# Twelve value column tiles of a gated linear attention layer by seven block products (Strassen) a pair, ahead of the heads

## The chip, the cores and the metric

The kernel runs on one core of one Trainium2 chip. The metric is the device time of one execution in microseconds (us). Five engines work beside each other, each through its own instructions in a fixed order: TensorE (PE: matmuls; PEld: the loading of their weights), VectorE (DVE), ScalarE (ACT), GpSimd (POOL) and SyncE (SP). SP's and POOL's queues also issue the transfers (DMA) between DRAM and the on-chip memory SBUF; matmuls write into PSUM. Engines wait for each other by semaphores.

## The reference

An encoder of two layers over 512 tokens of 2048 values, with 16 learned meta tokens ahead of them (528 columns in all). Each layer is h <- h + post_norm(mixer(pre_norm(h))). Layer 0 mixes by softmax attention. Layer 1 mixes by gated linear attention, with four heads, 256 key and 512 value channels each; what concerns the change is its input projection:

```python
proj = hp @ w_in          # w_in: 2048 x 6176
q, k, v, g_out, lr_f, lr_b = jnp.split(proj, [1024, 2048, 4096, 6144, 6160], axis=-1)
q = heads(q, GLA_HEAD_K) * (GLA_HEAD_K ** -0.5)
k, v = heads(k, GLA_HEAD_K), heads(v, GLA_HEAD_V)
o = o_f + o_b             # two gated scans over chunks, forward and backward
o = rmsnorm(o, o_norm)
return (o * jax.nn.silu(g_out)) @ w_out
```

All of it is float32. The values are 2048 columns of w_in: sixteen column tiles of 128.

## The kernel before

The kernel is one program, written out as Python. Activations lie with channels on the partitions and tokens along the free axis: u is 16 tiles (k = 0 to 15) of 128 x 528. A float32 product is made of three matmuls of a reduced kind: each operand is split into a high part (rounded, by a copy on ScalarE) and a low part (the rest, by a subtraction on VectorE), and hi x hi, hi x lo and lo x hi are added up in PSUM (split(), L130 to L132; three(), L153 to L156). uh and ul are the parts of u; weights() (L143) loads 512 KB of weights into a tile named wraw, of which there are two, and splits it into whi and wlo, of which there are three each, some 400 priorities ahead of the place where it stands.

project() (L158) makes one column tile of 128: in HALVES (twice 264 tokens) it is 2 x 16 x 3 = 96 matmuls of 264, in REAL (the 512 real tokens) 48 of 512. group() (L171) makes two column tiles at once in four banks of PSUM, with other work (extra) in each step k.

The order is set in two steps. A Clock in the Python program keeps a modelled time: project(), group() and the heads advance it, and side work, registered by clk.after() or as a generator by clk.drive(), is written out when the modelled time reaches it; clk.finish() writes out the rest of a generator at once. Then the framework orders the instructions of each engine by priorities; what stands in that order is fixed in the built program.

Around the change the work runs like this. At the end of layer 0 the output projection makes h tile by tile; squares() has ScalarE square each tile and GpSimd add it into acc (L649), mean_rsqrt() forms the norm (L661), and residual() (L665) makes h, in halves, and from it uh and ul. group() (L750) then makes the first two key tiles of layer 1 in ten steps that are split by halves, with the low-rank columns (plr) and the residual of the next tiles in it; token_major() (L695) transposes h (ht) and sums its squares by token. second_norm() (L760) makes the norm of layer 1: five small matmuls (mrow, L769) spread it over all partitions, each copied by ScalarE into r1row (L770), since all of them use one PSUM tile in turn. project() of the first q tile runs beside it, then lrf (L779) splits the low-rank columns by direction.

Then come four heads. Each makes two key and two query tiles (kf and qf, scaled by the norm: take_k L753, take_q L756), four value tiles (value_tile(), L964: project, copy to vt, transposes vps, copies times the norm into vh and vl) and four tiles of the output gate (gate_tile(), L990). Beside them go, as generators, gates() (L818: decays from the low-rank columns by the matmuls pz, L829), scores() (L872: chunk by chunk decayed queries and keys and their products, one item each "slot" of modelled us) and, a head later, outputs(). The normed, gated outputs go to DRAM (og_d), and the output projection ends the program.

## Time and profile before

| | us |
|---|---|
| runs (3), median | 1809.86 |
| runs, lowest to highest | 1809.09 to 1812.7 |
| the profiled execution | 1808.54 |
| its span, first to last instruction | 1806.8 |
| TensorE busy | 1784.1 (12855 matmuls) |
| VectorE / ScalarE / GpSimd busy | 1000.9 / 896.3 / 163.3 |
| mean granted TensorE clock | 0.998 |
| head 1 of layer 1 | 1151.24 to 1314.22, 163.0 long |

How to read it: a row of the timeline gives start, length, engine, line, operation and tile, and in brackets how long the engine stood idle before and what ended that. Starts count from the first instruction. Matmuls are pipelined, so their lengths overlap; the step from start to start is what one costs. A group's row gives its busy time and the mean length in ns, and behind the second bar the idle time ahead of its instructions. A row of the waits gives the line that waited, what ended the wait, the total in us, the times and the longest. A row of a stretch gives, for each engine, busy us and the number of instructions, then the granted clock, the share of DMA engines in use and GB/s. The page's rows of transfers end with the median us from issue to landing.

### The profile page before, as it was taken

The numbers are of one execution on the slowest core, as the hardware profiler recorded it, in microseconds if no ns is written. First come the engines' busy times: TensorE is split into PE (matmuls) and PEld (weight loads), VectorE is DVE, ScalarE is ACT, GpSimd is POOL, SyncE is SP. The second block draws the span as 40 slices with busy tenths as digits, with TensorE's granted clock in tenths as the row PEclk, the third lists the DMA queues.
The fourth block names the chain that finished last, engine by engine and source line by source line (L and its number), as shares of the span: only waits on it lengthen the run. The fifth ranks groups of instructions, "written<-read, shape, count | busy, mean of one in ns | idle before, by whom it ended". The sixth has DMA issues, their size and how long they took to land.

```text
span 1806.8 us, 31956 instructions
## 1 busy us (share of the span) xinstructions
PE 1784.1 (99%) x12855; PEld 1683.8 (93%) x12855; DVE 1000.9 (55%) x1985; ACT 896.3 (50%) x1869; POOL 163.3 (9%) x185
## 2 busy tenths in 40 slices
PE   8999999999999999999999999999999999999998
PEld 8899999999999999999999898998999899988886
DVE  5776565656565656632255575565456465654224
ACT  4555444444444454542346575566447454743221
POOL 3211111111111111211110000000000000000000
PEclk9999999999999999999999999999999999999999
DMA  8322223323233332433435232323223333434333
GB/s 273 103 67 76 84 87 86 91 80 91 81 91 84 91 113 81 143 106 93 117 118 174 71 84 80 94 73 92 80 85 85 92 88 91 126 117 175 93 94 128
DMA packets 262133, 184.24 MB, mean 102 GB/s; under 512 B 8460, under 2 KB 238160, under 8 KB 261456
## 3 DMA queue, kind: packets, MB, share of 16 engines
q1 hardware_dynamic: 257312, 165.78, 31.8%
q0 software_dynamic: 4672, 16.42, 2.5%
q8 instruction: 101, 1.65, 0.4%
q14 instruction: 48, 0.39, 0.1%
HBM read 156.03 MB, written 19.64 MB: 97 GB/s over the span
## 4 chain that ended last, share of the span: by engine, by line
PE 92%; DVE 2%; ACT 2%; DMA 1%; POOL 1%; issue 1%; SPq 0%; DVEq 0%; POOLq 0%; ACTq 0%
PE pp L154 22%; PE pp L156 22%; PE pp L155 21%; PE f L1057 2%; PE f L1055 2%; PE f L1056 2%; PE pT L492 2%; PE s L473 1%; PE s L474 1%; PE s L475 1%; PE o L935 1%; ACT whi L131 1%; PE o L934 1%; PE o L933 1%; DMA qs<-qw 1%; PE o L513 1%
## 5 line engine op out<-in xcount | busy, mean ns | idle before, releaser
L154 PE MATMUL pp<-uh,whi 128*128 128x264 f32 (+1 forms) x3024 | 913.4, 302 | 2.1 <-ACT acc L644 1.0
L156 PE MATMUL pp<-uh,wlo 128*128 128x264 f32 (+1 forms) x3024 | 903.1, 299 | 0.4 <-POOL wlo L279 0.3
L155 PE MATMUL pp<-ul,whi 128*128 128x264 f32 (+1 forms) x3024 | 901.4, 298 | 0.3 <-DVE ul L340 0.3
L154 PEld LDWEIGHTS pp<-uh,whi 128*128 128x128 f32 x3024 | 569.1, 188 | 20.7 <-ACT acc L644 1.2
L156 PEld LDWEIGHTS pp<-uh,wlo 128*128 128x128 f32 x3024 | 569.4, 188 | 17.1 <-POOL wlo L279 0.6
L155 PEld LDWEIGHTS pp<-ul,whi 128*128 128x128 f32 x3024 | 569.8, 188 | 16.1 <-DVE ul L340 0.5
L132 DVE TENSOR_TENSOR wlo<-wraw,whi 128x1024 fp32r<-128x1024 f32 (+1 forms) x254 | 310.1, 1222 | 366.1 <-ACT whi L131 360.7
L131 ACT CAST whi<-wraw 128x1024 fp32r<-128x1024 f32 (+1 forms) x254 | 264.3, 1042 | 405.0 <-PE pp L155 278.8
L482 ACT ACTIVATE pn<-s,mx 128x528 f32<-128x528 f32 (+1 forms) x72 | 50.3, 699 | 88.4 <-DVE mx L479 66.9
L1057 PE MATMUL f<-whi,ul 128*128 128x512 f32 x192 | 75.6, 394 | 0.0
L1055 PE MATMUL f<-whi,uh 128*128 128x512 f32 x192 | 75.5, 393 | 0.0
L1056 PE MATMUL f<-wlo,uh 128*128 128x512 f32 x192 | 75.3, 392 | 0.0
L225 POOL TENSOR_TENSOR qw<-qw,cos 128x528 f32<-128x528 f32 x24 | 31.8, 1326 | 372.8 <-DMA qs<-qw 339.0
L478 DVE TENSOR_REDUCE mx<-s 128x1 f32<-128x528 f32 (+1 forms) x72 | 50.8, 705 | 18.9 <-PE s L475 17.8
L960 POOL DMA_DIRECT2D og_d<-og x24 | 12.8, 542 | 492.9 <-DVE og L958 492.9
L497 DVE TENSOR_TENSOR pl<-pT,ph 128x512 fp32r<-128x512 f32 (+1 forms) x80 | 47.5, 593 | 4.8 <-ACT ph L496 3.8
L235 DVE TENSOR_TENSOR qw<-qw,qs 128x528 f32<-128x528 f32 x24 | 17.0, 707 | 59.2 <-POOL qs L226 59.2
L496 ACT CAST ph<-pT 128x512 fp32r<-128x512 f32 (+1 forms) x80 | 40.6, 507 | 16.2 <-PE pT L492 10.1
L1057 PEld LDWEIGHTS f<-whi,ul 128*128 128x128 f32 x192 | 36.1, 188 | 8.3
L1056 PEld LDWEIGHTS f<-wlo,uh 128*128 128x128 f32 x192 | 36.1, 188 | 8.3
L1055 PEld LDWEIGHTS f<-whi,uh 128*128 128x128 f32 x192 | 36.1, 188 | 8.1
L860 DVE TENSOR_TENSOR eq<-eq,qf 128x512 f32<-128x512 f32 (+1 forms) x56 | 34.4, 614 | 15.7 <-ACT eq L858 14.8
(335 smaller groups left out, 2766.0 us busy)
## 6 DMA issues: line engine op xcount, KB each, us to landing
wraw<-in_gla_w_in_dram SPq DMA_DIRECT2D x96, 512.0 KB, 3.9
wraw<-in_attn_w_in_dram SPq DMA_DIRECT2D x94, 512.0 KB, 3.9
wraw<-in_attn_w_out_dram SPq DMA_DIRECT2D x32, 512.0 KB, 3.8
wraw<-in_gla_w_out_dram SPq DMA_DIRECT2D x32, 512.0 KB, 3.8
qs<-qw SPq DMA_DIRECT2D x96, 66.0 KB, 2.8
h<-h_d SPq DMA_DIRECT2D x32, 132.0 KB, 2.4
h_d<-h POOLq DMA_DIRECT2D x16, 256.0 KB, 3.5
h_d<-hb SPq DMA_DIRECT2D x16, 256.0 KB, 2.8
```

Source lines behind the costliest of these rows:

```text
L131: A.copy(hi, src)
L132: V.tensor_tensor(lo, src, hi.bitcast(F32), op=ALU.subtract)
L154: PE.matmul(ps, wh, uh[:, k, a:b], start=first, stop=False)
L155: PE.matmul(ps, wh, ul[:, k, a:b], start=False, stop=False)
L156: PE.matmul(ps, wl, uh[:, k, a:b], start=False, stop=last)
L478: V.reduce_max(mx, s, axis=AX.XY)
L482: A.activation(pn[:, :T].rearrange("p (a b) -> p a b", a=2), s, AF.Exp, bias=mx, scale=SCALE, accum_out=sm)
L496: A.copy(ph[:, :, c:c + m], pt[:, :, qc:qc + m])
L497: V.tensor_tensor(pl[:, :, c:c + m], pt[:, :, qc:qc + m], ph[:, :, c:c + m].bitcast(F32), op=ALU.subtract)
L1055: PE.matmul(ps, uh[:, k, ts], wh[:, kk], start=(k == 0), stop=False)
L1056: PE.matmul(ps, uh[:, k, ts], wl[:, kk], start=False, stop=False)
L1057: PE.matmul(ps, ul[:, k, ts], wh[:, kk], start=False, stop=(k == KT - 1))
```

## The change

Strassen's scheme (in Winograd's form) makes a product of 2 x 2 blocks with seven block products in place of eight. Here the blocks are two column tiles of w_in (256 columns) by the two halves of the 2048 channels on one side, and the two halves of the channels by the two halves of the 528 tokens on the other. So a pair of value tiles takes seven products of 8 x 3 = 24 matmuls of 264, 168 in all.

What is new or moved:

- residual() also writes h to DRAM (hf_d), by GpSimd's queue, 32 transfers of 128 x 264.
- group() makes the first two value tiles, not the first two key tiles; ScalarE copies them to y tiles (four copies).
- combine() forms, once, the sums of blocks of u that the products need, T1 to T4: for each k of 8 it loads two tiles of h (three transfers), scales them on ScalarE, makes three subtractions on VectorE, and splits the result, 128 x 1056, into th and tl. It goes beside the first and second key tile and the first query tile, in four tiles x0 to x3 (in the build x_12374 to x_12377).
- seven() makes a pair: it loads four quarters of the weights (a11, a21, a22, a12, 512 KB each) into the tiles of a list of six (those four and two of wraw), forms three sums of them on VectorE ahead and one behind (L236), splits each product's weights, and makes the products (matmuls L242 to L244); the sums of the results go to the y tiles (copy L266, adds L249).
- token_rows() transposes a pair's y tiles (ten transposes, vps, L894), scales them on ScalarE, and writes them to DRAM (v_d) by GpSimd's queue. It is registered 1.0 of modelled time behind the pair.
- The first two key tiles and the first query tile go to DRAM by to_dram() (L863: the scaling on VectorE) and come back when the heads begin.
- In the heads, load_v() brings the values from DRAM; only the last two value tiles of head 3 are made there. The keys of the next head are made in the head before it (two buffers kfs). gates() loads its part of gk_up in each head, where before all of it was made ready at the end of layer 0. scores() takes a slot of 4.0 (3.6 in head 0) for 4.8.

```diff
@@ residual
         V.tensor_tensor(h, h, h0, op=ALU.add)
+        nc.gpsimd.dma_start(out=hf_d[k][:, a:b], in_=h)
         A.activation(hi, h, AF.Copy, scale=col(PRE + KT + k))
@@ new
+    def combine(th, tl, xs, src, scale):
+        def load(k):
+            if k < KH:
+                x = xs[k % len(xs)]
+                nc.sync.dma_start(out=x[:, :T], in_=src[k])
+                nc.sync.dma_start(out=x[:, T:T + HALF], in_=src[k + KH][:, HALF:])
+                nc.sync.dma_start(out=x[:, T + HALF:], in_=src[k + KH][:, :HALF])
+        for k in range(len(xs)):
+            load(k)
+        for k in range(KH):
+            x = xs[k % len(xs)]
+            A.activation(x[:, :T], x[:, :T], AF.Copy, scale=scale(k))
+            A.activation(x[:, T:], x[:, T:], AF.Copy, scale=scale(k + KH))
+            V.tensor_tensor(x[:, :T], x[:, HALF:HALF + T], x[:, :T], op=ALU.subtract)
+            V.tensor_tensor(x[:, T2:T4], x[:, T2:T4], x[:, :HALF], op=ALU.subtract)
+            V.tensor_tensor(x[:, T4:], x[:, T4:], x[:, T2:T4], op=ALU.subtract)
+            split(th[:, k], tl[:, k], x)
+            load(k + len(xs))
+            yield 2.4
...
+    def seven(src, c, ys, th, tl, free):
...
+        a11, a21, a22, s, a12, spare = free
+        for t, i, j in ((a11, 0, 0), (a21, 1, 0), (a22, 1, 1), (a12, 0, 1)):
+            quarter(t, i, j)
+        y1, y2 = ys
+        l, r = slice(0, HALF), slice(HALF, T)
+        w = parts(a11)
+        sums(s, a21, a22, ALU.add)
+        sums(a21, a11, a21)
+        sums(a11, s, a11)
+        A.copy(y1[:, l], product(w, of_u(0, 0)))
+        add(y1[:, r], product(parts(a11), of_t(T2)), y1[:, l])
+        add(y2[:, r], product(parts(a21), of_t(T3)), y1[:, r])
+        add(y2[:, l], product(parts(a22), of_t(T4)), y2[:, r])
+        p5 = product(parts(s), of_t(T1))
+        add(y2[:, r], p5, y2[:, r])
+        add(y1[:, r], p5, y1[:, r])
+        w = parts(a12)
+        sums(a11, a12, a11)
+        add(y1[:, l], product(w, of_u(1, 0)), y1[:, l])
+        add(y1[:, r], product(parts(a11), of_u(1, 1)), y1[:, r])
+        return [spare, a21, a22, s, a12, a11]
@@ between layer 0 and the heads
-    group([(w_in1, 1024, 256)], accs1, low_rank, halves=NB)
+    group([(w_in1, 2048, 256)], accs1, low_rank, halves=NB)
...
+    ys = y_tiles()
+    for i, ps, a, b in banks1:
+        A.copy(ys[i][:, a:b], ps)
...
-    project(w_in1, 0, REAL, lambda ps, a, b: take_q(0, ps, a, b))
+    to_dram(0, 1024, 1.0, HALVES)
...
+    built = clk.drive(combine(th, tl, quarters, hf_d, lambda k: col(PRE + KT + k)))
+    clk.after(1.0, lambda ys=ys: token_rows(ys, 0))
+    to_dram(1, 1024 + P, 1.0, HALVES)
+    to_dram(2, 0, 1.0 / 16, REAL)
+    clk.finish(built)
+    free = [q[:, :1024] for q in quarters]
+    free += [wpool.tile([P, 1024], F32, tag="wraw", name="wraw", bufs=2) for _ in range(2)]
+    for vc in range(2, 14, 2):
+        ys = y_tiles()
+        free = seven(w_in1, 2048 + vc * P, ys, th, tl, free)
+        clk.after(1.0, lambda ys=ys, vc=vc: token_rows(ys, vc))
+    clk.flush()
@@ heads
+        else:
+            sc = clk.drive(chain(gates(h), scores(h, 3.6)))
...
-            sc = clk.drive(scores(4.8))
...
-        for i in range(4):
-            value_tile(h, i)
+            sc = clk.drive(scores(h, 4.0))
+        vs = clk.drive(load_v(h))
+        for i in range(2):
+            if h < G_HEADS - 1:
+                project(w_in1, 1024 + (h + 1) * 256 + i * P, HALVES, lambda ps, a, b: take_k(h + 1, i, ps, a, b))
+            else:
+                if not i:
+                    clk.finish(vs)
+                value_tile(h, 2 + i)
```

## The prediction

> **What bounds the kernel now.** I read the page first: its span, the engines' shares and the chain that ended last.

> ```profile
> span 1806.8 us, 31956 instructions
> PE 1784.1 (99%) x12855; PEld 1683.8 (93%) x12855; DVE 1000.9 (55%) x1985; ACT 896.3 (50%) x1869; POOL 163.3 (9%) x185
> PE 92%; DVE 2%; ACT 2%; DMA 1%; POOL 1%; issue 1%; SPq 0%; DVEq 0%; POOLq 0%; ACTq 0%
> ```

> TensorE is busy for 99% and carries 92% of the chain, so a matmul taken out pays in full as long as TensorE keeps work to do. The second view is TensorE's waits:

> ```profile
> PE ssq L661 <- issue: 2.5, 1, 2.5
> ...
> PE vps L972 <- ACT z L830: 0.6, 1, 0.6
> ...
> PE pz L829 <- DVE vl L976: 0.4, 1, 0.4
> ```

> The largest wait of the whole run is 2.5 us. There is nothing to win but matmuls, and any new pause is a loss. Third, busy time by stretches: 100 us of products of 264 columns only, head 1 of layer 1, and its stage of scores.

> ```profile
> core 0: us, PE busy (x) PEld busy (x) DVE busy (x) ACT busy (x) POOL busy (x), PEclk, DMA share, GB/s
> 790.00:890.00 100.00, 100.00 (x825) 100.00 (x824) 21.12 (x18) 30.31 (x54) 16.18 (x17) 1.00 0.33 95
> 1151.24:1314.22 162.98, 162.98 (x1085) 149.66 (x1083) 91.50 (x163) 90.28 (x193) 4.27 (x8) 1.00 0.30 85
> 1188.00:1235.00 47.00, 47.00 (x385) 46.36 (x384) 31.32 (x59) 34.73 (x84) 0.00 (x0) 1.00 0.29 79
> ```

> The first row gives 100/825 = 0.1212 us for a matmul of 264 columns. In the scores ScalarE is busy for 34.73/47 = 74%, with TensorE still full.

> **The change part by part.** Each number below is added to the profiled execution's own 1808.54 us (its span of 1806.8 plus 1.7 around it); the median of the runs, 1809.86, is 1.3 us above that. A pair of column tiles was 2 x 96 matmuls of 264 and is now 7 x 24 = 168. Six pairs save 6 x 24 = 144 matmuls: 144 x 0.1212 = **-17.5 us**, on the path as long as TensorE waits for nothing.

> Against this stand the operations that feed the sevens. Their prices are taken from rows of VectorE and of ScalarE in head 1, and from the transfers on the page:

> ```profile
> L132 DVE TENSOR_TENSOR wlo<-wraw,whi 128x1024 fp32r<-128x1024 f32 x24 | 29.4, 1224 | 22.7 <-ACT whi L131 21.0 <-PE sm L869 1.6
> L754 DVE TENSOR_TENSOR kf<-pp,r1row 128x264 f32<-128x264 f32 x4 | 1.7, 432 | 2.3 <-PE pp L156 2.3
> L757 DVE SCALAR_TENSOR_TENSOR qf<-pp,r1row 128x512 f32<-128x512 f32 x2 | 1.4, 692 | 7.0 <-PE pp L156 7.0
> ```

> ```profile
> L131 ACT CAST whi<-wraw 128x1024 fp32r<-128x1024 f32 x24 | 25.0, 1044 | 36.3 <-PE pp L155 36.3
> L966 ACT COPY vt<-pp 128x264 f32<-128x264 f32 x8 | 3.0, 370 | 0.0
> ```

> ```profile
> wraw<-in_gla_w_in_dram SPq DMA_DIRECT2D x96, 512.0 KB, 3.9
> ```

> *Entry into the sevens, first product.* Before, VectorE has at this place (the second column tile of q, after the group) only the evacuation of q between two splits of weights that were loaded long ago:

> ```order
> 1008 L132 TENSOR_TENSOR wlo<-wraw,whi 128x1024
> 1009 L757 SCALAR_TENSOR_TENSOR qf<-pp,r1row 128x512
> 1010 L132 TENSOR_TENSOR wlo<-wraw,whi 128x1024
> 1011 L835 SCALAR_TENSOR_TENSOR z<-z,e 128x528
> 1012 L837 SCALAR_TENSOR_TENSOR bf<-ones,z 128x512
> 1013 L838 SCALAR_TENSOR_TENSOR bf<-ones,z 128x16
> ```

> Now VectorE has this from q's evacuation (L863) to the low part of the second product's weights. x_12374 to x_12377 are the four tiles in which combine() forms the sums of u; seven() loads its quarters a11, a21 and a22 into the first three of them and puts the sum s into the fourth.

> ```order
> 1028 L863 SCALAR_TENSOR_TENSOR y<-pp,r1row 128x512
> 1029 L135 TENSOR_TENSOR tl<-x_12374,th 128x1056
> ...
> 1037 L135 TENSOR_TENSOR wlo<-x_12374,whi 128x1024
> 1038 L135 TENSOR_TENSOR tl<-x_12376,th 128x1056
> 1039 L135 TENSOR_TENSOR tl<-x_12377,th 128x1056
> 1040 L236 TENSOR_TENSOR x_12377<-x_12375,x_12376 128x1024
> 1041 L236 TENSOR_TENSOR x_12375<-x_12374,x_12375 128x1024
> 1042 L236 TENSOR_TENSOR x_12374<-x_12377,x_12374 128x1024
> 1043 L135 TENSOR_TENSOR wlo<-x_12374,whi 128x1024
> ```

> The last reader of x_12374 moved behind q's evacuation, which waits for the last matmul of q; so a11 can be loaded only after that, and TensorE has no other work in its order than the sevens from here on. From q's end: evacuation 0.69, split of 1056 columns about 1.26 (1.224 x 1056/1024), transfer 3.9, high part 1.04, low part 1.22, together 8.1; the first two matmuls don't need the low part (0.24). So TensorE idles **7.9 us** (7 to 9; 3.9 is a median, and neither end of this chain is overlapped by anything). In the same way a22 goes into x_12376, whose last reader stands behind the low part of a11 (row 1038). From there: split 1.26, transfer 3.9, three sums 3 x 1.22 = 3.7, high part 1.04, low part 1.22, together 11.1. The first product, 24 x 0.1212 = 2.9, and the 0.24 lie beside it: **7.9 us** (5 to 9.5; the lower end if the sum into a11 is started by an earlier landing). What hides this in the kernel before are weights loaded a tile ahead; that cover is gone for these two products only, since from the second pair on the quarters land in tiles that came free a pair earlier.

> *The clock after an idle stretch.* TensorE's timeline around its longest wait, and the granted clock behind it in two stretches:

> ```profile
> 945.42 0.28 PE L155 MATMUL g<-ul,whi 128*128 128x264 f32 x1
> 948.17 1.12 PE L661 MATMUL ssq<-acc,ones 128*128 128x264 f32 x2 [2.46 <-issue]
> ...
> 950.62 0.42 PE L156 MATMUL g<-uh,wlo 128*128 128x264 f32 x1
> 950.85 0.42 PE L685 MATMUL plr<-uh,wl 128*128 128x264 f32 x1
> ```

> ```profile
> 948.17:951.50 3.33, 3.33 (x11) 2.92 (x12) 2.57 (x6) 2.96 (x9) 0.00 (x0) 0.51 0.57 163
> 951.84:960.00 8.16, 8.16 (x71) 8.16 (x70) 7.53 (x21) 6.85 (x17) 0.00 (x0) 1.00 0.85 261
> ```

> After 2.46 us of idling the granted clock was 0.51 for 3.33 us and matmuls started 0.23 us apart: a loss of 3.33 x 0.49 = **1.6 us**. Both idle stretches here are longer, but a slow first product only eats into the second stretch, which VectorE sets; so it is paid once (0 to 3.3). [...]

> *First keys and second norm.* TensorE's five mrow matmuls, each of which waits until ScalarE has copied the one ahead, before (five of TensorE's rows) stood between products of 512 columns:

> ```profile
> 994.57 0.49 PE L769 MATMUL mrow<-dg,ones 128*128 128x128 f32 x2
> 994.81 0.48 PE L155 MATMUL pp<-ul,whi 128*128 128x512 f32 x1
> ...
> 995.41 0.49 PE L769 MATMUL mrow<-dg,ones 128*128 128x128 f32 x2
> ...
> 996.25 0.49 PE L769 MATMUL mrow<-dg,ones 128*128 128x128 f32 x2
> ...
> 997.10 0.40 PE L769 MATMUL mrow<-dg,ones 128*128 128x16 f32 x2
> ```

> In TensorE's order before there are two to four such products between any two of them:

> ```order
> 7631 L769 MATMUL mrow<-dg,ones 128x128
> 7632 L155 MATMUL pp<-ul,whi 128x512
> 7633 L156 MATMUL pp<-uh,wlo 128x512
> 7634 L769 MATMUL mrow<-dg,ones 128x128
> 7635 L154 MATMUL pp<-uh,whi 128x512
> 7636 L155 MATMUL pp<-ul,whi 128x512
> 7637 L769 MATMUL mrow<-dg,ones 128x128
> ```

> Now, in the first key tile, they stand at the transposes of the first value pair (vps, of its tiles y_12176 and y_12177):

> ```order
> 7655 L894 MATMUL vps<-ident,y_12177 128x128
> 7656 L894 MATMUL vps<-ident,y_12176 128x128
> 7657 L853 MATMUL mrow<-dg,ones 128x128
> 7658 L894 MATMUL vps<-ident,y_12177 128x128
> 7659 L853 MATMUL mrow<-dg,ones 128x128 x3
> 7660 L157 MATMUL pp<-uh,whi 128x264
> 7661 L853 MATMUL mrow<-dg,ones 128x16
> ```

> Between the first and the fifth lie four steps of 0.84 = 3.4 us, of which four mrow (0.24 each, 994.57 to 994.81) and two other matmuls fill 1.2: 2.2 us of idling. Ahead of it four new copies of y (0.37 each) stand on ScalarE in front of the evacuation of the token-major transposes: about 1.1 of 1.5 shows; the second lrf matmul waits some 0.3. Together **+3.5 us** (1 to 5).

> *Steady sevens.* A pair takes TensorE 168 x 0.1212 = 20.4 us and ten transposes. VectorE has 7 splits and 5 sums of 1.22 and 7 adds of 0.43, some 17.7 us; ScalarE 7 x 1.04 plus a few copies. TensorE stays the bound. But the ten transposes of a pair stand 57 - 48 = 9 matmuls (1.1 us) behind its last product, and the add they need stands on VectorE behind a low part and a sum of the next pair. That low part takes the third buffer, free at the end of the sixth product: 1.04 + 1.22 + 1.22 + 0.43 = 3.9 against 2.9 + 1.1 = 4.0, with four hand-overs between engines in it. I take 0.4 for each of six pairs, **+2.5 us** (0 to 8).

> *Heads.* Four value tiles leave each of heads 0 to 2 and two leave head 3; the side work (gates, scores, outputs) loses splits and copies of value tiles with them, and gets loads of v from DRAM, whose splits of 128x512 are some 0.7 each, four in a head. The waits of 0.6 and 0.4 quoted above fall away, -1.0; the first gate matmul now waits for its late load, +0.3. Score items follow faster (slot 4.0, 3.6 in head 0, where 4.8 was), so ScalarE's 74% becomes at most 74 x 4.8/4.0 = 89%: below 100 still. In head 3 the first items bunch, as the loads of v are finished at a stroke there: +1.0. Together **+0.3** (-1 to +7).

> Sum: -17.5 + 7.9 + 7.9 + 1.6 + 3.5 + 2.5 + 0.3 = **+6.2**; 1808.5 + 6.2 = 1814.7, so **1815 us**.

> **The rivals.** *One stall only (faster).* The second load is early: a22's place comes free before the first product's weights are ready, so that only the three sums stand between the first product's weights and the second's (3.7 + 1.04 + 1.22 - 2.9 - 0.24 = 2.8), and the transposes are covered, with 1.5 left of the mrow pauses: -17.5 + 7.9 + 2.8 + 1.6 + 1.5 - 1.0 = -4.7: 1803.8. Against it stands row 1038; for it, that durations decide whether anything idles. It decides if the second idle stretch is under 3 us. Chance 0.15.

> *The entry eats the gain and nothing else does (same).* The mrow pauses cost their low end of 1.0, transposes and heads nothing, and the two stretches 15 together: -17.5 + 15 + 1.6 + 1.0 = 0.1: 1808.6. For it: TensorE's order has few other waits today. Chance 0.2.

> *ScalarE late in the heads (slower still).* In heads 0 and 3 items come faster than ScalarE makes them; one of the 16 or so items late by 0.4 us each gives 6 us: 1821. It decides where ScalarE is above 95% busy in the stretch of scores. Chance 0.15.

> *GpSimd's queue.* Its last add of squares now stands behind transfers of h to DRAM:

> ```profile
> 930.92 0.82 POOL L649 TENSOR_TENSOR acc<-acc,sq 128x264 f32<-128x264 f32 x1 [11.74 <-ACT sq L647]
> 940.87 2.99 POOL L649 TENSOR_TENSOR acc<-acc,sq 128x264 f32<-128x264 f32 x1 [9.14 <-ACT sq L647]
> ```

> The add ends at 943.9 and is wanted at 945.7 by the matmul quoted above, which then waited until 948.17 for something else; 4.3 us are free, so it costs nothing unless two transfers take 2.99 each like the second add: 2 x 2.99 + 0.8 - 4.3 = 2.5, so 1817. [...] Chance 0.05.

> **How the numbers follow.** The forecast's own case (1812 to 1818) has 0.45. A measurement here tells 0.2% (3.6 us) from no change: faster is below 1806.2, slower above 1813.5. Faster: 0.15. Same: 0.2 and 0.07 of the forecast's case, 0.27. Slower: 0.38 + 0.15 + 0.05 = 0.58. The range, 1803 to 1823, takes in the one-stall case and most of the late-ScalarE case; all unknown costs at their low ends give 1803, at their high ends 1833, of which I leave out the upper part as unlikely together.

> **What would show it.** In the profile after: two idle stretches of TensorE of about 8 us each, at the first two products of the first pair, the first ended by VectorE's low part behind a load, and a granted clock near half behind them; waits at mrow of about 0.6 each; waits below 1 us at the transposes of L894; 20.4 us between pairs. The forecast is wrong if either stretch is under 4 us, or if the heads' waits together are over 5 us.

## The result and the profile after

The change made the kernel slower: 1840.86 us (median of 4, 1833.45 to 1843.47) against 1811.28 (median of 4, 1809.09 to 1814.17). The ratio is 1.0156, 95% interval 1.0122 to 1.0189. The forecast was 1815, range 1803 to 1823: the side was right, the size was not, 30 us for the 6 that the sum gave. Even with every cost at its high end the prediction came to 1833 only.

The page of the changed kernel, span, shares and chain. The profiled execution is the slowest of the four, 1843.47.

```profile
span 1841.7 us, 32124 instructions
PE 1787.2 (97%) x12711; PEld 1677.4 (91%) x12711; DVE 1064.3 (58%) x2053; ACT 926.6 (50%) x1872; POOL 198.1 (11%) x253
PE 59%; issue 32%; POOL 3%; DVE 3%; ACT 2%; DMA 1%; SPq 0%; POOLq 0%; DVEq 0%; ACTq 0%
```

TensorE does 144 matmuls fewer (12711 for 12855), as forecast, and yet is busy for longer: among other things, at half clock 24 matmuls were busy for 5.45 us (below), where 2.9 was usual. The larger of its waits in layer 1 (ssq, which waited for 2.9 where it was 2.5 before, and the rows of layer 0, which differ from before by 1 us at most, are left out):

```profile
PE pp L242 <- ACT whi L134: 14.8, 2, 9.7
...
PE ht L785 <- ACT hb L787: 2.8, 1, 2.8
...
PE pz L968 <- DVE r L1093: 2.2, 3, 1.0
PE sso L1091 <- ACT z L969: 2.1, 3, 0.7
PE vps L894 <- DVE y L249: 1.6, 5, 0.8
...
PE sso L1091 <- DVE acc L1088: 1.3, 2, 0.7
PE ss L1007 <- ACT hq L134: 1.1, 3, 0.5
PE mrow L853 <- DVE dg L851: 1.1, 1, 1.1
...
PE mrow L853 <- ACT r1row L854: 1.0, 3, 0.4
...
PE sm L1007 <- ACT hq L134: 0.9, 1, 0.9
```

Before, no wait behind ssq was over 0.6. The entry's two stretches (14.8, forecast 15.8), mrow and vps were in the forecast; sso, sm, ss and most of pz were not, and of ht only the 1.1 us for ScalarE's copies.

TensorE's timeline at the first two products, and the granted clock in four stretches there (from just before q's end to the first product, the first product, to the second, the second):

```profile
1048.30 0.59 PE L242 MATMUL pp<-uh,whi 128*128 128x264 f32 x1 [9.69 <-ACT whi L134]
...
1059.59 0.59 PE L242 MATMUL pp<-th,whi 128*128 128x264 f32 x1 [5.11 <-ACT whi L134]
```

```profile
1038.10:1048.30 10.20, 0.51 (x3) 0.07 (x1) 8.53 (x17) 6.44 (x10) 0.54 (x1) 0.78 0.79 234
1048.30:1054.20 5.90, 5.45 (x24) 5.14 (x24) 3.54 (x3) 1.90 (x2) 0.00 (x0) 0.52 0.33 92
1054.20:1059.59 5.39, 0.28 (x3) 0.07 (x1) 3.69 (x4) 1.47 (x3) 0.00 (x0) 0.80 0.00 0
1059.59:1063.00 3.41, 3.27 (x13) 2.96 (x14) 3.41 (x4) 1.85 (x2) 0.00 (x0) 0.50 0.02 5
```

The first product ran at a clock of 0.52 and took 5.9 us for 2.9 (some 0.5 of it a wait for its own low part), and the second stretch is shorter by just that: 5.1 + 3.0 = 8.1, where 7.9 was forecast. VectorE over the same time:

```profile
1038.28 1.32 DVE L212 TENSOR_TENSOR x<-x 128x528 f32<-128x528 f32 x2
1039.52 0.77 DVE L213 TENSOR_TENSOR x<-x 128x264 f32<-128x264 f32 x2
1040.21 0.77 DVE L214 TENSOR_TENSOR x<-x 128x264 f32<-128x264 f32 x2
1040.89 0.68 DVE L863 SCALAR_TENSOR_TENSOR y<-pp,r1row 128x512 f32<-128x512 f32 x1
1041.82 2.43 DVE L135 TENSOR_TENSOR tl<-x,th 128x1056 fp32r<-128x1056 f32 x2 [0.25 <-ACT th L134]
...
1048.28 1.22 DVE L135 TENSOR_TENSOR wlo<-x,whi 128x1024 fp32r<-128x1024 f32 x1 [1.42 <-ACT whi L134]
1049.43 2.42 DVE L135 TENSOR_TENSOR tl<-x,th 128x1056 fp32r<-128x1056 f32 x2
1054.72 3.74 DVE L236 TENSOR_TENSOR x<-x,x 128x1024 f32<-128x1024 f32 x3 [2.87 <-issue]
```

The chain is the one of the forecast, evacuation, split, landing, split, sums. It begins 2.3 us behind q's end (1048.30 - 9.69 = 1038.61, to 1040.89), because combine()'s own sums (L212 to L214) are late and stand ahead of the evacuation: that is where 9.7 comes from in place of 7.9.

### The profile page after: what moved, and what is told of

Read it like the earlier page. It is cut to its first block, busy times and chain, and to the rows that moved or that the text cites. A ratio compares the mean times of both kernels' runs of the same rounds, so it can differ in the third digit from the quotient of the medians.

```text
span 1841.7 us, 32124 instructions
## 1 busy us (share of the span) xinstructions
PE 1787.2 (97%) x12711; PEld 1677.4 (91%) x12711; DVE 1064.3 (58%) x2053; ACT 926.6 (50%) x1872; POOL 198.1 (11%) x253
## 4 chain that ended last, share of the span: by engine, by line
PE 59%; issue 32%; POOL 3%; DVE 3%; ACT 2%; DMA 1%; SPq 0%; POOLq 0%; DVEq 0%; ACTq 0%
PE pp L157 13%; PE pp L159 13%; PE pp L158 13%; PE f L1223 2%; PE f L1221 2%; PE f L1222 2%; PE pT L582 2%; POOL v_d L899 1%; PE s L563 1%; PE s L564 1%; PE s L565 1%; PE o L603 1%; PE o L602 1%; PE o L604 1%; ACT whi L134 1%
## 5 line engine op out<-in xcount | busy, mean ns | idle before, releaser
L157 PE MATMUL pp<-uh,whi 128*128 128x264 f32 (+1 forms) x2640 | 803.9, 305 | 0.3 <-ACT sq L303 0.3
L159 PE MATMUL pp<-uh,wlo 128*128 128x264 f32 (+1 forms) x2640 | 795.0, 301 | 0.3 <-POOL wlo L369 0.3
L158 PE MATMUL pp<-ul,whi 128*128 128x264 f32 (+1 forms) x2640 | 794.6, 301 | 0.2 <-DVE ul L430 0.2
L159 PEld LDWEIGHTS pp<-uh,wlo 128*128 128x128 f32 x2640 | 498.3, 189 | 17.4 <-POOL wlo L369 0.6
L157 PEld LDWEIGHTS pp<-uh,whi 128*128 128x128 f32 x2640 | 497.9, 189 | 16.9 <-ACT sq L303 0.5
L158 PEld LDWEIGHTS pp<-ul,whi 128*128 128x128 f32 x2640 | 498.9, 189 | 14.1 <-DVE ul L430 0.5
L135 DVE TENSOR_TENSOR wlo<-wraw,whi 128x1024 fp32r<-128x1024 f32 (+1 forms) x245 | 298.5, 1219 | 358.8 <-ACT whi L134 358.7
L134 ACT CAST whi<-wraw 128x1024 fp32r<-128x1024 f32 (+1 forms) x245 | 255.1, 1042 | 358.9 <-PE pp L158 207.4
L242 PE MATMUL pp<-th,whi 128*128 128x264 f32 x192 | 55.9, 291 | 5.3 <-ACT whi L134 5.1
L243 PE MATMUL pp<-tl,whi 128*128 128x264 f32 x192 | 55.4, 289 | 0.0
L244 PE MATMUL pp<-th,wlo 128*128 128x264 f32 x192 | 55.1, 288 | 0.0
L242 PE MATMUL pp<-uh,whi 128*128 128x264 f32 x144 | 42.5, 295 | 9.7 <-ACT whi L134 9.7
## 6 DMA issues: line engine op xcount, KB each, us to landing
wraw<-in_attn_w_in_dram SPq DMA_DIRECT2D x94, 512.0 KB, 4.0
wraw<-in_gla_w_in_dram SPq DMA_DIRECT2D x81, 512.0 KB, 3.9
wraw<-in_attn_w_out_dram SPq DMA_DIRECT2D x32, 512.0 KB, 3.9
wraw<-in_gla_w_out_dram SPq DMA_DIRECT2D x32, 512.0 KB, 3.8
x<-in_gla_w_in_dram SPq DMA_DIRECT2D x15, 512.0 KB, 4.2
```

The source lines that it names most:

```text
L134: A.copy(hi, src)
L135: V.tensor_tensor(lo, src, hi.bitcast(F32), op=ALU.subtract)
L157: PE.matmul(ps, wh, uh[:, k, a:b], start=first, stop=False)
L158: PE.matmul(ps, wh, ul[:, k, a:b], start=False, stop=False)
L159: PE.matmul(ps, wl, uh[:, k, a:b], start=False, stop=last)
L242: PE.matmul(ps, w[0][:, k], bh[:, k], start=k == 0, stop=False)
```

## The experiments

All times are medians; each run was timed beside the kernel before (1811 to 1812 in all of them). The expectations speak of the changed kernel's 1841.

The four runs of the changed kernel span 10 us, and the intervals of most single edits overlap its own, so a gain of 3 to 8 us in a median is not shown by the median alone. Each edit is therefore also read in its own stage of the profiled executions. The *heads* reach from the first matmul behind the sevens to the first one of the output projection: 510.0 us in the changed kernel, 510.0 to 511.6 in the six traces (its own among them) with the same heads. The *norm* reaches from the second ssq matmul to the last mrow matmul: 54.9 in the changed kernel, 52.0 to 56.0 in the eight traces without an edit that bears on it. The *entry and sevens* follow up to the heads: 183.5 in the changed kernel, 180.8 to 185.1 in the seven without an edit there. The part ahead of the second ssq matmul, which no edit touches but for a start-up tile in the last two, takes 945.4 to 950.3 in the 17 traces, in the changed kernel 950.3.

**The openings of heads 1 to 3.** The gates of a head and the outputs of the head before run beside each other there, and the matmuls pz and sso share one PSUM tile, which a wait of either blocks for the other. The change put a load and 2.0 of modelled time ahead of the gates. The edit gives the outputs the same:

```diff
     def outputs(h, slot):
+        if h < G_HEADS - 1:
+            yield 2.0
```

> The outputs of heads 0 to 2 start 2.0 of modelled time later, so that they stand to the gates of the next head as they did before the change (the new load of gk_up put the gates 2.0 later). Theory (the sso and pz matmuls share one PSUM tile, and the shift makes them collide): the waits of sso (3.4 us in the waits view) and most of pz's at DVE r (2.2 us) in the openings of heads 1 to 3 go, and with the refill behind each about 8 us of the 1841: 1832 to 1835. Rival (the opening is too short, 22 us of query tiles where 45 us of keys and queries stood, so that ScalarE and VectorE are late): the waits stay in sum, 1839 to 1842.

Measured: 1836.8, ratio to before 1.0137 (1.0120 to 1.0154). TensorE's timeline at the same place of head 1's opening, of the changed kernel and of this one:

```profile
1301.26 0.29 PE L968 MATMUL pz<-lr,ups 80*128 80x264 f32 x1
...
1305.45 0.70 PE L1091 MATMUL sso<-acc,ones 128*128 128x256 f32 x2 [0.72 <-ACT z L969]
...
1306.67 0.38 PE L968 MATMUL pz<-lr,ups 80*128 80x264 f32 x1
```

```profile
1300.63 0.28 PE L968 MATMUL pz<-lr,ups 80*128 80x264 f32 x1
...
1301.48 0.70 PE L1093 MATMUL sso<-acc,ones 128*128 128x256 f32 x2
```

The rows of sso and of pz behind VectorE are gone from the waits, with as much work in as short an opening as ever: the theory holds, the rival falls. The saving, 4.1 in the median, is half of what I expected; the waits come to 5.6, and the heads are 5.3 us shorter in the trace (504.7 for 510.0).

**The scores' density.** The rival for the heads:

```diff
-            sc = clk.drive(chain(gates(h), scores(h, 3.6)))
+            sc = clk.drive(chain(gates(h), scores(h, 4.8)))
...
-            sc = clk.drive(scores(h, 4.0))
+            sc = clk.drive(scores(h, 4.8))
```

> The scores' slots back to 4.8 in all heads, nothing else. Theory (in heads 0 to 2 the density of scores costs little, the losses stand in the openings): the waits at sso and pz stay, and what the slots don't fit into the shorter heads is finished at a stroke at the end: 1842 to 1850. Rival (ScalarE is late because score items come too fast): waits at ss and sm fall, 1836 to 1839.

Measured: 1841.3 (1.0159, 1.0143 to 1.0174), no change, and none in the heads (511.1); ss and sm still wait for 1.2 and 0.9. Density was not the cause, and the longer slots show no cost either, so my theory's price for them was wrong as well.

**Head 3.**

```diff
-                if not i:
-                    clk.finish(vs)
-                value_tile(h, 2 + i)
-        for i in range(4):
+                gate_tile(h, i)
+                if i:
+                    clk.finish(vs)
+                    for n in range(2):
+                        value_tile(h, 2 + n)
+        for i in range(2 if h == G_HEADS - 1 else 0, 4):
```

> In head 3 two gate tiles come ahead of the two value tiles, so that the loads of v are spread and nothing is finished at a stroke there. Theory (bunching): the waits at sm and ss in head 3 (2.1 us, with refill and clock 4 us in the stretch from 1556 to 1580) go: 1836 to 1838. Rival (ScalarE is too busy there whatever the order): they move to another place of head 3, 1840 to 1842.

Measured: 1837.6 (1.0140, 1.0121 to 1.0158), 3.3 less. The trace bears it out: the wait at sm, 0.9 in the changed kernel, is gone, that at ss is down from 1.1 to 0.5, and the heads take 506.5 for 510.0, 3.5 less, as the theory has it.

**The wait at ht.** ScalarE evacuates the token-major rows of h into two buffers (hb), which transfers take to DRAM. In the changed kernel ScalarE stood idle for them seven times, before the change four times. The rows of the tile's view, of the kernel before and of the changed one:

```profile
  DMA h_d<-hb: 5.2, 4
...
DMA to landing us min/median/max: 2.2/2.8/5.4
```

```profile
  DMA h_d<-hb: 10.8, 7
...
DMA to landing us min/median/max: 2.0/4.2/6.8
```

Two edits: the new writes of h to DRAM left out (combine() then reads h of layer 0), and more buffers.

```diff
-        nc.gpsimd.dma_start(out=hf_d[k][:, a:b], in_=h)
...
-    built = clk.drive(combine(th, tl, quarters, hf_d, lambda k: col(PRE + KT + k)))
+    built = clk.drive(combine(th, tl, quarters, h0_d, lambda k: col(PRE + KT + k)))
```

> Leaves out the 32 transfers that write h to DRAM; combine() reads h of layer 0 instead, so the twelve Strassen tiles are of other values. Theory (these writes slow the landing of the token-major rows of h, for which ScalarE then waits, and TensorE behind it): the wait of 2.8 us at ht goes, with the slow clock behind it 4 to 5 us: 1836 to 1837. Rival (ScalarE's order is what delays it, or GpSimd's queue delays the second norm): ht's wait stays, or the ssq wait of 2.9 goes instead.

```diff
-        hb = t2.tile([P, 512], F32, tag="hb", name="hb")[:n]
+        hb = t2.tile([P, 512], F32, tag="hb", name="hb", bufs=4)[:n]
```

> Four buffers in place of two for the token-major rows on their way to DRAM. Theory (as for the run without the writes of h): the transfers land as late as in the changed kernel, but nobody waits; ht's wait of 2.8 us goes, 1836 to 1838. Rival (the delay is not the landing): no change, 1839 to 1842.

Measured: 1837.4 (1.0143, 1.0128 to 1.0158) without the writes, 1832.6 (1.0117, 1.0093 to 1.0142) with four buffers. The same view of the two runs:

```profile
  DMA h_d<-hb: 8.2, 5
...
DMA to landing us min/median/max: 2.2/3.2/5.5
```

```profile
DMA to landing us min/median/max: 2.4/4.6/6.6
```

Without the writes the rows land in 3.2; in the eight kernels with the writes and two buffers the median is 4.1 or 4.2 each time. With four buffers they land as late as 4.6, and nobody waits. So the writes cost time by how they slow the rows' landing, not by GpSimd's queue, which four buffers leave as it is. The wait at ht alone is no measure of it: it is 0.5 without the writes, but 0.7 in the run of head 3 too, where nothing was changed there. The norm is: 51.2 without the writes, just below the 52.0 to 56.0 of the others, and 46.4 with four buffers (47.6 to 48.0 in the six kernels below that have them). So the buffers are worth some 6 us, and the median's 8.2 is above that. It is more than the wait at ht, since with the rows out early the mrow matmuls no longer stand together (the waits of 1.1 and 1.0 there are gone from its view).

**The entry: tiles, cover, clock.** First, the first pair's a11 and a21 go into wraw tiles, which are free early:

```diff
-    free = [q[:, :1024] for q in quarters]
-    free += [wpool.tile([P, 1024], F32, tag="wraw", name="wraw", bufs=2) for _ in range(2)]
+    free = [wpool.tile([P, 1024], F32, tag="wraw", name="wraw", bufs=2) for _ in range(2)]
+    free += [q[:, :1024] for q in quarters]
```

> The list of tiles is turned: the first pair's a11 and a21 go into the two wraw tiles, which are free early, and a22, s and a12 into tiles of combine(). Theory (the place of a11 sets the first idle stretch, VectorE's sums the second): the first product starts right behind q (its wait of 9.7 us goes to under 1), and the second stretch grows from 5.1 to 10 or 11 us, since the rest of the splits of combine() now stands in it; together 4 to 6 us less: 1835 to 1837. Rival (combine()'s own chain on ScalarE and VectorE is what is late, whatever the tiles): the sum of the two stretches stays at 15 us, 1840 to 1842.

Measured: 1835.1 (1.0132, 1.0115 to 1.0148). The first stretch went, the second grew to 13.0, 2 to 3 us more than I had: a11's tile was one cause, combine()'s late chain the other. The two waits fell by 1.8 us only, and the stage by 4.7 (178.8 for 183.5), so that the median came out as forecast is in part luck. Second, more work ahead of the sevens:

```diff
     to_dram(2, 0, 1.0 / 16, REAL)
+    to_dram(3, P, 1.0 / 16, REAL)
...
-    nc.sync.dma_start(out=qf[:, 0], in_=kq_d[2][:, :SEQ])
+    for i in range(2):
+        nc.sync.dma_start(out=qf[:, i], in_=kq_d[2 + i][:, :SEQ])
...
-        for i in range(0 if h else 1, 2):
+        for i in range(2 if h else 0):
             project(w_in1, h * 256 + i * P, REAL, lambda ps, a, b: take_q(i, ps, a, b))
```

> The second query tile of head 0 is made ahead of the sevens too (by way of DRAM like the first), so that TensorE has 11 us of work while the quarters land. Theory: the first idle stretch (9.7) goes, the second is left with q's evacuation, three sums and one split behind it, 0.7 + 3.7 + 2.3 - 2.9 = 3.8 us; with the clock 12 to 14 us less than the 1841, but head 0 loses 11 us of cover for its gates and scores (+2 to +4): 1829 to 1832. Rival (what is late is combine()'s chain, and it only moves behind the second query tile): stretches of 10 us or more stay, 1838 to 1843.

Measured: 1835.6 (1.0127, 1.0110 to 1.0144). Neither forecast has it: the two stretches fell from 14.8 to 6.4, but only 5.2 of these 8.4 us reached the end. I had expected 2 to 4 of them to be lost in head 0, whose query tile is gone, and the trace agrees: the heads take 501.3, 8.7 less, where the 48 matmuls that left them take 11.1 (48 steps of 0.232), so 2.4 are lost there. Third, work that nobody needs, to keep the clock up:

```diff
+        def warm(n):
+            if c != 2048 + 2 * P:
+                return
+            wp = ps_v.tile([P, 512], F32, tag="v", name="wps")[:, :HALF]
+            for i in range(n):
+                PE.matmul(wp, uh[:, 0, :P], uh[:, 0, :HALF], start=i == 0, stop=i == n - 1)
...
+        warm(70)
         A.copy(y1[:, l], product(w, of_u(0, 0)))
+        warm(55)
```

> Adds 125 matmuls of 264 whose result nobody reads, 70 ahead of the first product and 55 ahead of the second, so that TensorE is busy in the two idle stretches. Theory (the stretches are set by VectorE and transfers, and the slow clock behind them is paid once, behind the second): idle time turns into busy time, the granted clock stays at 1.0, and 2 to 3 us are saved: 1838 to 1839. Rival (the clock costs nothing beyond the waits, or the added matmuls delay the products): 1840 to 1845.

Measured: 1842.1 (1.0163, 1.0148 to 1.0179): nothing saved, and the stage takes 184.4 for 183.5. Both products still waited for ScalarE (1.4 and 0.4), so the added matmuls delayed neither. The clock did stay at 1.00 (the second product's stretch):

```profile
1057.90:1061.50 3.60, 2.85 (x21) 2.64 (x22) 3.60 (x4) 1.84 (x2) 0.00 (x0) 1.00 0.04 9
```

At full clock the second product waits for its low part instead, as VectorE is busy for all of the 3.60 us: behind the entry VectorE sets the pace, and the slow TensorE costs nothing measurable there.

**The transposes.**

```diff
-        clk.after(1.0, lambda ys=ys, vc=vc: token_rows(ys, vc))
+        clk.after(2.0, lambda ys=ys, vc=vc: token_rows(ys, vc))
```

> The transposes of a pair are registered 2.0 of modelled time behind it in place of 1.0, so that they stand about 9 matmuls later. Theory (the add they wait for is 0.2 to 0.9 us late at each pair): the five waits at vps, 2.4 us from start to start, go: 1838 to 1839. Rival (the y tiles or PSUM are then held longer and delay the next pair): 1841 or more.

Measured: 1841.4 (1.0162, 1.0147 to 1.0177). The five waits of 1.6 us became one of 0.3, and the time didn't move beyond its scatter, which is too wide to bound the term. From the first pair's last product to the heads the trace has 109.2 us; the ten kernels with the old place have 109.9 to 111.5, the five below with the transposes at 1.6 have 109.0 to 109.4. So the term is worth about 1.

**Together.** The outputs, head 3 and the four buffers in one kernel:

> Three of the single edits together: four buffers for the token-major rows, outputs 2.0 later, and in head 3 two gate tiles ahead of the value tiles. Theory (three separate causes): their gains add up, 8.2 + 4.1 + 3.3 us off the 1841: 1825. Rival (they share what they save, so that one wait takes another's place): 1829 to 1832.

Measured: 1819.3 (1.0045, 1.0031 to 1.0058). That is 21.6 off, more than the 15.6 of the three alone. The stages show why: the heads take 500.6 us, 9.4 less, where the two edits alone gave 5.3 and 3.5; the norm takes 48.0, 6.9 less. So the gains add up, to some 16 us, and none takes another's saving. Of the rest, the trace has 4.9 us ahead of ssq, which none of the three edits touches. The waits that stay are the entry's above all:

```profile
PE pp L242 <- ACT whi L134: 14.7, 2, 9.5
PE ssq L744 <- issue: 2.0, 1, 2.0
PE pt L428 <- DMA xt<-in_x_dram: 1.6, 1, 1.6
```

**The entry covered, step by step.** From here each kernel keeps the edits ahead of it. The first adds the second query tile, a tile of the first pair's own (qt), and puts the product of a12, which needs no sum of blocks, in second place (the diff leaves out the second query tile, shown above, the transposes at 1.6, and head 0's first gate matmul 2.0 later):

```diff
+    first_quarter = ta.tile([P, 1024], F32, name="qt")
...
+    free = [first_quarter] + [wpool.tile([P, 1024], F32, tag="wraw", name="wraw", bufs=2) for _ in range(2)]
+    free += [quarters[i][:, :1024] for i in (1, 0, 2)]
...
         A.copy(y1[:, l], product(w, of_u(0, 0)))
+        p6 = product(parts(a12), of_u(1, 0))
         add(y1[:, r], product(parts(a11), of_t(T2)), y1[:, l])
+        add(y1[:, l], p6, y1[:, l])
```

> The three edits, and the entry: the second query tile of head 0 ahead of the sevens by way of DRAM; the first pair's quarters in one tile of its own and in the two wraw tiles; the product of a12 with u, which needs no sum of blocks, as the second one of each pair; transposes 1.6 behind the pair; the first gate matmul of head 0 2.0 later. Theory (the entry's two idle stretches come from tiles and from combine()'s own chain, and both are covered now): no wait over 2 us at the first pair, 1825 less 15 to 18, plus 2 to 4 for head 0's lost cover: 1809 to 1813, beside the kernel before; with everything covered, 1805. Rival (VectorE's order, not the tiles, keeps the second stretch): 1816 to 1822.

Measured: 1808.6 (0.9986, 0.9978 to 0.9995). The gain of the 144 matmuls begins to show. A wait of 2.5 stayed, where under 2 was forecast, at the second product:

```profile
1044.84 0.39 PE L242 MATMUL pp<-uh,whi 128*128 128x264 f32 x1 [2.50 <-ACT whi L134]
```

Then a12 changed places with a22:

```diff
-    free += [quarters[i][:, :1024] for i in (1, 0, 2)]
...
+    x0, x1, x2 = [q[:, :1024] for q in quarters[:3]]
+    free = [first_quarter, w0, x0, x1, w1, x2]
```

> As the run with all edits, but the first pair's a12 goes into the second wraw tile and a22 into a tile of combine(), so that the second product's weights are split ahead of the second query tile's evacuation. Theory (the 2.5 us that stayed at the first pair come from a12 landing in a late tile): that wait and the 0.8 at its low part go, 1805 to 1806. Rival (the wait moves to the third product, whose sum needs a22): 1808 to 1809.

Measured: 1810.6 (0.9992, 0.9983 to 1.0001). The rival, though its time was 2 us too low: the wait moved to the third product, and grew to 4.1. And head 0, with the same entry:

```diff
-        yield 2.0 if h else 4.0
+        yield 2.0 if h else 6.0
...
-            sc = clk.drive(chain(gates(h), scores(h, 3.6)))
+            sc = clk.drive(chain(gates(h), scores(h, 3.3)))
```

> As the run before it in this list, and in head 0 the first gate matmul 2.0 of modelled time later and the scores' slot 3.3 in place of 3.6. Theory (gk_up for head 0 lands in memory that the sevens free, so it is late whatever the order asks for): the wait of 1.7 us at pz goes, but the items follow faster, ScalarE and VectorE are late at ss: within 1.5 us of the run before it. Rival (only the asked order is too early): 2 to 3 us faster than it.

Measured: 1809.7 (0.9990, 0.9981 to 0.9999), within 1.5 of the run ahead of it, but that does not show the theory: pz's wait at gk_up fell from 1.5 to 0.8 only, ss waits hardly longer (1.8 for 1.6), and the heads are 2.1 shorter in the trace (489.9 for 492.0), which speaks for the rival; the first pair's wait grew from 4.1 to 5.3 beside it. Next a second tile, for which a start-up tile was given up:

```diff
+    firsts = [ta.tile([P, 1024], F32, name=f"qt{i}") for i in range(2)]
...
-    free = [first_quarter, w0, x0, x1, w1, x2]
+    free = [firsts[0], firsts[1], w0, x0, w1, x1]
```

> As the last run, but with a second tile of the first pair's own (the room comes from a small tile of the start, which now shares the tile of parameter rows), so that all four quarters of the first pair land early. Theory (in the entry only landings and sums behind late tiles are left): the wait of 5.3 us at the first pair goes to under 1, 1804 to 1806. Rival (combine()'s last splits are late themselves, behind the second query tile's evacuation): 3 us or more stay at the second or third product, 1807 to 1809.

Measured: 1811.5 (0.9998, 0.9987 to 1.0009), slower than either forecast. 6.5 us of waiting stood at the second product, now not for weights but for a PSUM bank. TensorE's row, and VectorE's rows ahead of it:

```profile
1046.18 0.56 PE L242 MATMUL pp<-uh,whi 128*128 128x264 f32 x1 [6.47 <-DVE y L863]
```

```profile
1042.12 1.22 DVE L236 TENSOR_TENSOR qt<-wraw,qt 128x1024 f32<-128x1024 f32 x1
1043.26 1.21 DVE L135 TENSOR_TENSOR wlo<-qt,whi 128x1024 fp32r<-128x1024 f32 x1
1044.39 0.42 DVE L214 TENSOR_TENSOR x<-x 128x264 f32<-128x264 f32 x1
1044.73 0.70 DVE L212 TENSOR_TENSOR x<-x 128x528 f32<-128x528 f32 x1
1045.35 0.68 DVE L863 SCALAR_TENSOR_TENSOR y<-pp,r1row 128x512 f32<-128x512 f32 x1
```

VectorE never rests there, and the evacuation of a query tile stands behind sums and splits that it does for later products. So the last edit takes the two evacuations off it:

```diff
+            if n >= 2:
+                A.activation(y[:, a:b], ps, AF.Copy, scale=scale)
+                G.tensor_tensor(y[:, a:b], y[:, a:b], r1row[:, a:b], op=ALU.mult)
+            else:
+                V.scalar_tensor_tensor(y[:, a:b], ps, scale, r1row[:, a:b], op0=ALU.mult, op1=ALU.mult)
```

> As the run before, but the two query tiles ahead of the sevens are evacuated by ScalarE and scaled by GpSimd, so that no PSUM bank waits for VectorE's place in the order. Theory (VectorE's order was what kept the 6.5 us: q's evacuation stood behind sums and splits): the wait at the first pair goes to under 2, and it is the first version clear of the kernel before, 1803 to 1806. Rival (the entry is bound by VectorE's and ScalarE's work itself, whatever the order): a wait of 4 us or more at another product, 1808 to 1811.

Measured: 1806.7 (0.9978, 0.9967 to 0.9989), the fastest of all, faster than the kernel before by 0.2% and than the changed one. The theory holds in the main: the wait for the bank is gone, and the time lies just above the forecast's 1806, but what is left at the first pair is 2.4 where under 2 was forecast, at the third product, for the high part of a sum of blocks:

```profile
1048.65 0.59 PE L242 MATMUL pp<-th,whi 128*128 128x264 f32 x1 [2.38 <-ACT th L134]
```

The kernel before, 1812.4 beside this run, less 17.5 would be 1794.9; the remaining 12 us were not taken apart by runs. The last column of the table below says where they stand in the trace: most of them in the heads.

## Why the prediction was right on the side and wrong on the size

What each stage loses is its length less its matmuls at their median steps (0.121 us for one of 264 columns, 0.232 for 512): an estimate, worked out from the traces, which holds waits, slow clock and refills together (at full clock the first matmul of 264 behind a wait of over 0.3 us took 0.39 us where 0.28 was usual, medians of 7 such waits before and of 5 in the changed kernel). The forecast's terms stand beside it, in us:

| stage | forecast | before | changed | three edits together | last edit |
|---|---|---|---|---|---|
| norm: second ssq matmul to last mrow | +3.5 | 3.3 | 10.7 | 3.6 | 3.7 |
| entry and sevens: last mrow to the heads | +19.9 | | 26.9 | 24.3 | 7.9 |
| heads, to the output projection | +0.3 | | 19.7 | 10.3 | 12.1 |
| the last two stages together | +20.2 | 4.9 | 46.6 | 34.6 | 20.0 |

So the changed kernel loses 7.4 us more in the norm and 41.7 more behind it; less 17.4 for the matmuls, with 3.0 ahead of ssq, that makes 34.7 of the 34.9 between the two profiled executions.

- *144 matmuls, -17.5.* Right in the count (17.4 by the median steps); the last run shows that the gain can be had in part.
- *The entry, 7.9 + 7.9.* Right in the mechanism, and the two stretches are 9.7 and 8.1 (with the first product's slow clock in it). The part that I took as early, combine()'s chain, was 2.3 late. The whole stage loses 7 us more than its terms; what else is in that was not taken apart.
- *The clock, +1.6, once.* The clock did fall to half for both products, but its price there is none that can be measured: the run with the added matmuls saved nothing. Not in the sum are two more slow stretches of 3.41 us each in the changed kernel, behind the waits at ht and at mrow (978.90 to 982.31 and 1006.20 to 1009.62, clock 0.50).
- *First keys and second norm, +3.5.* This step failed: the stage loses 7.4 more than before. It counted ScalarE's copies and the steps of the mrow matmuls (3.4 us from the first to the fifth, as it came out), but not that the rows' transfers would land late beside 32 new writes to DRAM (a median of 4.2 us where 2.8 was): for the rows ht waits, and through VectorE's dg the first mrow (1.1). I had put these writes down as a rival, for GpSimd's queue, at 5 in 100, and priced the instructions in the queue, not the traffic. With four buffers the stage is some 6 us shorter and loses about what it lost before.
- *Sevens, +2.5.* Right: 1.6 + 0.8 of waits at vps, and about 1 us less with the transposes later.
- *Heads, +0.3 (at most +7).* This step failed most: the heads lose 19.7 us, where the kernel before loses 4.9 in all from the last mrow on. TensorE's waits there come to 10.2, twice the 5 that was named as a sign of being wrong. It counted what each head does and how dense the score items stand, and the run with the old slots shows that density costs nothing. What it left out is the load of gk_up as a shift: 2.0 of modelled time in front of one generator moved it against another with which it shares a PSUM tile (5.3 in the trace). It also took head 3's bunch for 1.0 where 3.5 was measured. What the heads lose beyond these two stays open; in the trace of the three edits over half of the remaining 10.3 stands ahead of head 1's first gate matmul.
- With the three edits the kernel is 8 us above the kernel before, close to the sum's 6.2, but that is luck: the norm then loses 0.3 more than before where 3.5 was forecast, and the heads still lose far more than 0.3. *ScalarE late in the heads*, the rival that gave 1821, was right that the heads lose several us and wrong on the reason.

In the part of the program that the change does not touch the profiled executions differ too: in the first 750 us 6039 matmuls start in the kernel before and 6007 in the changed one, 32 x 0.1212 = 3.9 us, while another of these kernels (the run with the old slots) reaches 6041. So a part of the 34.9 between the two profiled executions is no effect of the change; the medians, 29.6 apart, are the measure.

## What to carry to other kernels

Where generators share one buffer, a delay ahead of one of them is a change of phase: list the shared tiles and who holds each at the place where something was shifted. Price a new transfer by whose landing it slows (here from 2.8 to 4.2 us), not only by its instruction. And when the bound engine loses work, the next one (VectorE here) becomes the pace at the seams: covering one late step there moved the wait to the next one three times, until VectorE itself was given less to do. Where medians scatter by as much as an edit is worth, measure the edit in its own stage of the trace, against the same stage of kernels that leave it alone.

## What the runs showed of the hardware that was not expected

In these traces the half clock did not follow from the length of the idling alone, but from how it fell into a grid of 3.41 us. In the kernel before, 2.46 us of idling ahead of ssq were followed by 3.33 us at 0.51, as the prediction quotes; in the run with four buffers 2.49 us at the same place were followed by a clock of 1.00 (TensorE's row, then the stretch behind it):

```profile
949.17 0.68 PE L744 MATMUL ssq<-acc,ones 128*128 128x264 f32 x2 [2.49 <-issue]
```

```profile
949.17:952.50 3.33, 3.33 (x24) 3.11 (x25) 2.73 (x6) 3.33 (x10) 0.54 (x1) 1.00 1.06 392
```

```profile
944.86:948.27 3.41, 0.95 (x8) 0.77 (x8) 2.54 (x7) 2.31 (x5) 0.00 (x0) 1.00 1.01 326
948.27:951.68 3.41, 3.41 (x12) 3.00 (x13) 2.63 (x6) 3.04 (x9) 0.00 (x0) 0.50 0.59 169
```

With four buffers it falls into two windows, 0.93 and 1.55. In the run with the later transposes even 3.20 us of idling at this place cost no clock, since they fall into two windows as 1.80 and 1.40:

```profile
943.98:947.39 3.41, 1.61 (x12) 1.40 (x12) 2.04 (x6) 1.05 (x4) 1.28 (x3) 1.00 1.06 378
947.39:950.80 3.41, 2.01 (x12) 1.82 (x13) 2.57 (x5) 3.22 (x7) 0.54 (x1) 1.00 0.99 367
```

Over the 17 traces, from 30 us on, all 43 windows at full clock with 1.81 us of idling or more were followed by a slow one (one of 2.46 in the kernel before, four of 2.51 to 3.41 in the changed one). Of the 335 with 0.30 to 1.56 only four were, all at the mrow matmuls (in the changed kernel with 1.13 us of idling, from 1002.79 on); of the ten between the two bounds, four. So in these traces 1.81 us of idling, a little over half a window, was enough where it fell into one.
